# First products in another order, PLE's last weight splits behind the x parts, and the first norm tile in two pieces

## The chip, the core and the metric

The kernel runs on one NeuronCore of a Trainium2 chip. The metric is the device time of one execution in microseconds (us). The engines in the rows are TensorE (PE; its weight loads are PEld), VectorE (DVE), ScalarE (ACT), GpSimd (POOL) and SyncE (SP). A row that ends in "q" (ACTq, SPq) is the issue of a DMA from that engine's queue.

## The reference, cut to what matters

A two-layer decoder trunk on 256 tokens of width 1024, in float32:

```python
def swiglu(x, w_gate, w_up, w_down):
    return (jax.nn.silu(x @ w_gate) * (x @ w_up)) @ w_down

for i in range(DEPTH):                      # DEPTH = 2
    x = layer_norm(DN_ALPHA * x + 0.5 * swiglu(x, ffn_w_gate[i, 0], ...), ln_g[i, 0], ln_b[i, 0])
    mix = mixer_ab(x, ...) if i % 2 == 0 else mixer_cd(x, ...)
    x = layer_norm(DN_ALPHA * x + mix, ln_g[i, 1], ln_b[i, 1])
    x = layer_norm(DN_ALPHA * x + 0.5 * swiglu(x, ffn_w_gate[i, 1], ...), ln_g[i, 2], ln_b[i, 2])
    x = x + jax.nn.sigmoid(x @ ple_w_gate[i]) * (p[i] @ ple_w_proj[i])
```

D_FF is 2816. The mixers project x with one combined weight matrix, run their recurrences on the pieces, and project back with a second one.

## The kernel before, in words

**Split products.** Each float32 operand is split into a high and a low part, and a product is three matmuls: high by high, high by low, low by high (`mm3`, L69). Of the weights, ACT casts the high part (`wh`, L61) and DVE subtracts it to get the low part (`wl`, L62). Of the activations, x is transposed by PE into a PSUM tile, ACT casts the high part out of it (`xh`, L112) and DVE makes the low part (`xl`, L113), both in `split_xT`.

**Weights.** All weights are one stream of units of 128x2048 (1 MB). `Weights.unit` (L45) takes the next one: SP loads it into a staging tile `wst` (two buffers), and each half of it becomes a pair wh_n_0, wl_n_0 and wh_n_1, wl_n_1. The names in the rows below carry the unit's number. `behind` (L90, and the table `g.w.behind`) adds an ordering edge: the cast and the split of unit n may not be placed before the named instruction on the same engine. `layer_norm` (L145) uses it to put unit `at + 1 + t` behind the split of its own tile t. Apart from such edges, the order on each engine comes from a scheduler that places the instructions when the kernel is built, after its own estimates of when each can start; each engine then runs its list in that order.

**One half-layer.** The 256 tokens are two tiles (t = 0, 1) of 128. `ffn_body` (L198) makes the gate and up products of 11 column groups f, the hidden activations, and the down products into four PSUM accumulators, and ends in `layer_norm` (L117) of both tiles. `layer_norm` adds the residual (`r_ln`, L126), takes mean and variance (L129, L131; the power -0.5 on POOL, L81), subtracts and scales by the first row (L136) and makes x by the second (`x_ln`, L138), 512 columns at a time. Each half of 512 columns is transposed by four PE instructions into one PSUM tile (`tp_ln`, L142, tag "tr", two buffers for the whole kernel) and split. The next half-layer's first products need these splits.

**First products.** `run_tiles` (L163) makes one 128x512 output group for both token tiles out of two weight units (kh = 0, 1: rows k = 0 to 3 and 4 to 7 of x). With `tile_major` it runs all 24 products of tile 0 and then those of tile 1, so that tile 0 can start before tile 1 is normalised. It is used for f = 0 of each of the four feed-forward layers (`gu_f`) and for the first projection of each mixer (`pj_u` after norm 0, `pj_hq` after norm 3). For each half unit of rows, the products of xh with wh and wl come first and those of xl with wh last (L176).

**PLE.** `ple` (L280) makes the gate of the per-layer embedding in two column halves c for both tiles; `finish` (L297) applies it to x, transposes the 512 columns and splits them for the next layer. The last layer (`last`) has no such split. The places that the text speaks of are called after the norm or layer: ln0 to ln5 are the six norms (`ln3` is the first norm of the second layer), `ple0` is the first PLE, and f00, f01, f10, f11 are the feed-forward layers. Of the rest of the kernel, `nws_glr` (L595) is the high part of a small weight `nw_glr` of the second mixer, loaded on ACT's DMA queue (L591).

## Time and profile before

| | |
|---|---|
| three timed runs | 1224.89, 1226.21, 1229.82 us; median 1226.21 |
| the profiled execution | 1226.01 us, of which the span from first to last instruction is 1224.2 |
| PE busy | 1189.6 us, 97% of the span |
| DVE, ACT busy | 852.3 us (70%), 588.5 us (48%) |
| HBM traffic | 219.56 MB read, 12.06 MB written, 189 GB/s over the span |

The profile is one execution. A timeline row gives the start and the length of an instruction, what it writes and reads, and, in brackets, how long its engine sat idle before it and what ended that. Matmul lengths overlap: a 128x512 product is listed with 0.39 us but the next one starts 0.23 us after it. The column PEclk is the share of TensorE's full clock that was granted in a stretch: 1.00 is 2.4 GHz, 0.50 is 1.2 GHz.

### The profile page before, as it was taken

How to read it: one execution, taken by the hardware profiler on the slowest of the kernel's cores; microseconds unless marked ns; L12 is line 12 of the kernel's file. 1: busy time of each engine (PE TensorE's matmuls, PEld its weight loads, DVE VectorE, ACT ScalarE, POOL GpSimd, SP SyncE). 2: the span in 40 equal slices, each digit the busy share in tenths (PEclk: the TensorE clock that was granted, in tenths of full speed). 3: DMA queues.
4: the chain of work that ended last, by engine and by line, in shares of the span. 5: the costliest groups of instructions: out<-in, count | busy, mean ns of one | idle time of the engine just before them, and what ended most of it. 6: DMA issues, size and time to landing. Idle time of an engine off the chain costs nothing.

```text
span 1224.2 us, 17248 instructions
## 1 busy us (share of the span) xinstructions
PE 1189.6 (97%) x6786; PEld 987.4 (81%) x6786; DVE 852.3 (70%) x1352; ACT 588.5 (48%) x870; POOL 73.2 (6%) x126
## 2 busy tenths in 40 slices
PE   8999999999999999999999999999999999999998
PEld 6887777798878878888887888887888868888886
DVE  6999874779999675554576545456689876555566
ACT  5644443444666434444434444443575535444434
POOL 0011112120212000000000000000100100000000
PEclk9999999899999999999999999999999999999999
DMA  7567667587744546555526555554633327555532
GB/s 282 207 228 257 223 205 290 211 271 239 198 122 143 192 153 226 201 176 194 203 95 240 196 190 188 185 193 158 241 113 128 104 99 254 176 202 174 203 138 103
DMA packets 44609, 232.74 MB, mean 190 GB/s; under 512 B 9680, under 2 KB 10352, under 8 KB 20848
## 3 DMA queue, kind: packets, MB, share of 16 engines
q1 hardware_dynamic: 30672, 206.06, 48.5%
q0 software_dynamic: 4688, 14.16, 3.7%
q10 hardware_dynamic: 9168, 11.42, 2.9%
q8 instruction: 53, 0.87, 0.3%
q14 instruction: 28, 0.23, 0.1%
HBM read 219.56 MB, written 12.06 MB: 189 GB/s over the span
## 4 chain that ended last, share of the span: by engine, by line
PE 67%; DVE 10%; DMA 2%; ACT 2%; issue 1%; ACTq 0%; DVEq 0%
PE gu_f L178 29%; PE acc_f L72 5%; PE acc_f L70 5%; PE acc_f L71 5%; DVE wl L62 3%; DMA wst<-in_wall_dram 1%; PE acc_ab L72 1%; PE acc_ab L70 1%; PE acc_ab L71 1%; PE ht_f L215 1%; PE pj_u L178 1%; PE pj_hg L178 1%; PE pj_gr L178 1%; PE pj_hi L178 1%; PE pj_gv L178 1%
## 5 line engine op out<-in xcount | busy, mean ns | idle before, releaser
L62 DVE TENSOR_TENSOR wl<-wst,wh 128x1024 fp32r<-128x1024 f32 (+1 forms) x378 | 453.0, 1217 | 258.2 <-ACT wh L61 251.0
L61 ACT CAST wh<-wst 128x1024 fp32r<-128x1024 f32 (+1 forms) x378 | 385.9, 1045 | 349.2 <-PE acc_f L72 104.6
L70 PE MATMUL acc_f<-wh,hh_f 128*128 128x512 f32 x352 | 137.3, 391 | 1.9 <-ACT wh L61 1.4
L71 PE MATMUL acc_f<-wl,hh_f 128*128 128x512 f32 x352 | 137.5, 392 | 0.0
L72 PE MATMUL acc_f<-wh,hl_f 128*128 128x512 f32 x352 | 135.2, 392 | 0.0
L70 PEld LDWEIGHTS acc_f<-wh,hh_f 128*128 128x128 f32 x352 | 66.1, 188 | 15.8 <-ACT wh L61 1.6
L178 PE MATMUL gu_f<-wh,xh_in 128*128 128x512 f32 x176 | 71.9, 413 | 6.0 <-ACT wh L61 6.0
L72 PEld LDWEIGHTS acc_f<-wh,hl_f 128*128 128x128 f32 x352 | 66.1, 188 | 13.7
L71 PEld LDWEIGHTS acc_f<-wl,hh_f 128*128 128x128 f32 x352 | 66.1, 188 | 13.5
L178 PE MATMUL gu_f<-wh,xh_ple 128*128 128x512 f32 x176 | 70.8, 402 | 2.6 <-ACT xh_ple L112 2.6
L178 PE MATMUL gu_f<-wh,xh_ab 128*128 128x512 f32 x176 | 69.8, 396 | 0.5 <-ACT xh_ab L112 0.5
L178 PE MATMUL gu_f<-wl,xh_in 128*128 128x512 f32 x176 | 70.2, 402 | 0.0
L178 PE MATMUL gu_f<-wl,xh_ab 128*128 128x512 f32 x176 | 68.8, 391 | 1.3 <-DVE wl L62 1.3
L178 PE MATMUL gu_f<-wh,xh_cd 128*128 128x512 f32 x176 | 69.9, 397 | 0.0
L178 PE MATMUL gu_f<-wl,xh_ple 128*128 128x512 f32 x176 | 69.6, 396 | 0.0
L178 PE MATMUL gu_f<-wl,xh_cd 128*128 128x512 f32 x176 | 68.8, 391 | 0.7 <-DVE wl L62 0.7
L211 ACT ACTIVATE sg_f<-gu_f 128x256 f32<-128x256 f32 x88 | 33.7, 383 | 69.1 <-PE gu_f L178 67.8
L178 PE MATMUL gu_f<-wh,xl_ab 128*128 128x512 f32 x176 | 66.9, 391 | 0.0
L178 PE MATMUL gu_f<-wh,xl_cd 128*128 128x512 f32 x176 | 66.8, 391 | 0.0
L178 PE MATMUL gu_f<-wh,xl_ple 128*128 128x512 f32 x176 | 66.7, 391 | 0.0
L178 PE MATMUL gu_f<-wh,xl_in 128*128 128x512 f32 x176 | 66.6, 392 | 0.0
L212 DVE TENSOR_TENSOR sg_f<-sg_f,gu_f 128x256 f32<-128x256 f32 x88 | 36.8, 418 | 27.8 <-ACT sg_f L211 27.7
(469 smaller groups left out, 2348.9 us busy)
## 6 DMA issues: line engine op xcount, KB each, us to landing
wst<-in_wall_dram SPq DMA_DIRECT2D x185, 1024.0 KB, 4.8
row<-in_lnr_dram SPq DMA_DIRECT2D x12, 512.0 KB, 6.4
s5d<-s5pk POOLq DMA_DIRECT2D x8, 704.0 KB, 4.3
tab<-s5d ACTq DMA_DIRECT2D x8, 384.0 KB, 4.7
Q<-s5d ACTq DMA_DIRECT2D x8, 320.0 KB, 4.5
wst<-in_wall_dram SPq DMA_DIRECT2D x4, 512.0 KB, 6.7
s5d<-s5W POOLq DMA_DIRECT2D x8, 256.0 KB, 2.5
W<-s5d ACTq DMA_DIRECT2D x8, 256.0 KB, 4.0
```

What stands on the lines that cost most here:

```text
L61: ops = [nc.scalar.copy(wh[:, c], src[:, c])]
L62: ops.append(nc.vector.tensor_tensor(wl[:, c], src[:, c], f32(wh[:, c]), op=ALU.subtract))
L70: nc.tensor.matmul(out, xh, wh, start=first, stop=False)
L71: nc.tensor.matmul(out, xh, wl, start=False, stop=False)
L72: nc.tensor.matmul(out, xl, wh, start=False, stop=last)
L178: nc.tensor.matmul(ps[t], x, w, start=kh == 0 and i == 0, stop=kh == 1 and i == len(mms) - 1)
L211: nc.scalar.activation(sg, ps[t][:, 0:256], AF.Silu)
L212: nc.vector.tensor_tensor(sg, sg, ps[t][:, 256:512], op=ALU.mult)
L215: nc.tensor.transpose(tp[:, k, :], sg[:, k * P:(k + 1) * P], g.ident)
```

## The change

Three edits. (1) In `run_tiles` with `tile_major`, the 24 products of a tile are put in three lists: xh by wh of all eight rows of x together with xh by wl of the first unit; then xl by wh of all eight; then xh by wl of the second unit. (2) In `ple`'s `finish` for c = 1, the next weight units but one are put behind the x split of tile 0 and tile 1 (for the first PLE: units 100 and 101). (3) In `layer_norm`, the first 512 columns of tile 0 are scaled, transposed and split in two pieces of 256 columns; both pieces go into one PSUM tile. The parameter n of `layer_norm` is renamed, since n is now the number of blocks in a piece.

```diff
--- before.py
+++ after.py
@@ -104,20 +104,20 @@
     return [x[:, k, t * P:(t + 1) * P] for x in xT]
 
 
-def split_xT(g, t, half, src, xT):
-
-    nc = g.nc
-    s = slice(4 * half, 4 * half + 4)
+def split_xT(g, t, half, src, xT, part=slice(0, 4)):
+
+    nc = g.nc
+    s = slice(4 * half + part.start, 4 * half + part.stop)
     h, l = (x[:, s, t * P:(t + 1) * P] for x in xT)
     a = nc.scalar.copy(h, src)
     b = nc.vector.tensor_tensor(l, src, f32(h), op=ALU.subtract)
     g.anchors = a.ins, b.ins
 
 
-def layer_norm(g, n, t, acc, coef, xT):
-
-    nc = g.nc
-    name = f"ln{n}_{t}"
+def layer_norm(g, ln, t, acc, coef, xT):
+
+    nc = g.nc
+    name = f"ln{ln}_{t}"
     r = g.lnp.tile([P, D], F32, tag="ln_r", name=f"r_{name}")
     st = g.small.tile([P, 2, 6], F32, tag="ln_st", name=f"st_{name}")
     half = [slice(512 * h, 512 * h + 512) for h in range(2)]
@@ -133,14 +133,17 @@
     x = g.xp.tile([P, D], F32, tag=f"x{t}", name=f"x_{name}")
     for h in range(2):
         s = half[h]
-        nc.vector.scalar_tensor_tensor(r[:, s], r[:, s], mv[:, 0:1], g.grow[n][0][:, s], op0=ALU.subtract,
+        nc.vector.scalar_tensor_tensor(r[:, s], r[:, s], mv[:, 0:1], g.grow[ln][0][:, s], op0=ALU.subtract,
                                        op1=ALU.mult)
-        op = nc.vector.scalar_tensor_tensor(x[:, s], r[:, s], rstd, g.grow[n][1][:, s], op0=ALU.mult, op1=ALU.add)
-        g.scaled = (op.ins,)
         tp = g.ps.tile([P, 4, P], F32, tag="tr", name=f"tp_{name}_{h}", bufs=2)
-        for k in range(4):
-            nc.tensor.transpose(tp[:, k, :], x[:, (4 * h + k) * P:(4 * h + k + 1) * P], g.ident)
-        split_xT(g, t, h, tp, xT)
+        n = 4 if t or h else 2
+        for k0 in range(0, 4, n):
+            c = slice((4 * h + k0) * P, (4 * h + k0 + n) * P)
+            op = nc.vector.scalar_tensor_tensor(x[:, c], r[:, c], rstd, g.grow[ln][1][:, c], op0=ALU.mult, op1=ALU.add)
+            g.scaled = (op.ins,)
+            for k in range(k0, k0 + n):
+                nc.tensor.transpose(tp[:, k, :], x[:, (4 * h + k) * P:(4 * h + k + 1) * P], g.ident)
+            split_xT(g, t, h, tp[:, k0:k0 + n, :], xT, slice(k0, k0 + n))
     g.x[t] = x
     g.w.behind[g.w.at + 1 + t] = g.anchors
 
@@ -172,16 +175,26 @@
             c = slice(512 * (j % 2), 512 * (j % 2) + 512)
             h, l = of_tile(xT, t, k)
             mms += [(h, wh[:, c]), (h, wl[:, c]), (l, wh[:, c])]
-        if tile_major:
-            mms = [m for i, m in enumerate(mms) if i % 3 < 2] + mms[2::3]
         for i, (x, w) in enumerate(mms):
             nc.tensor.matmul(ps[t], x, w, start=kh == 0 and i == 0, stop=kh == 1 and i == len(mms) - 1)
 
     if tile_major:
         units = [g.w.unit() for kh in range(2)]
         for t in range(NT):
-            for kh in range(2):
-                part(kh, t, units[kh])
+            mms = [[], [], []]
+            for k in range(KT):
+                wh, wl = units[k // 4][k % 4 // 2]
+                c = slice(512 * (k % 2), 512 * (k % 2) + 512)
+                h, l = of_tile(xT, t, k)
+                mms[0].append((h, wh[:, c]))
+                if k < 4:
+                    mms[0].append((h, wl[:, c]))
+                else:
+                    mms[2].append((h, wl[:, c]))
+                mms[1].append((l, wh[:, c]))
+            mms = sum(mms, [])
+            for i, (x, w) in enumerate(mms):
+                nc.tensor.matmul(ps[t], x, w, start=i == 0, stop=i == len(mms) - 1)
         return
     for kh in range(2):
         pieces = g.w.unit()
@@ -310,6 +323,8 @@
         for k in range(4):
             nc.tensor.transpose(tp[:, k, :], xn[t][:, (4 * c + k) * P:(4 * c + k + 1) * P], g.ident)
         split_xT(g, t, c, tp, xT)
+        if c:
+            g.w.behind[g.w.at + 1 + t] = g.anchors
 
     for kh in range(2):
         units[0][kh] = g.w.unit()
```

The scheduler places the instructions anew around these edits. Three places follow. The first is PE from the transposes of norm 3's tile 0 (`tp_ln3_0_0` is its first 512 columns, `tp_ln3_0_1` its second) into the mixer's first projection `pj_hq_0`; wh_132, wl_132 are the first weight unit, wh_133, wl_133 the second. Before:

```order
L142 MATMUL tp_ln3_0_0_7784<-cs_217,x_ln3_0_7781 128x128 x4
L142 MATMUL tp_ln3_0_1_7793<-cs_217,x_ln3_0_7781 128x128 x4
L178 MATMUL pj_hq_0_7867<-wh_132_0_7871,xh_f10_7743 128x512
L178 MATMUL pj_hq_0_7867<-wl_132_0_7872,xh_f10_7743 128x512
...
L178 MATMUL pj_hq_0_7867<-wh_132_1_7875,xh_f10_7743 128x512
L178 MATMUL pj_hq_0_7867<-wl_132_1_7876,xh_f10_7743 128x512
...
L178 MATMUL pj_hq_0_7867<-wh_132_0_7871,xl_f10_7744 128x512 x2
L178 MATMUL pj_hq_0_7867<-wh_132_1_7875,xl_f10_7744 128x512 x2
L178 MATMUL pj_hq_0_7867<-wh_133_0_7881,xh_f10_7743 128x512
L178 MATMUL pj_hq_0_7867<-wl_133_0_7882,xh_f10_7743 128x512
```

and with the change:

```order
L145 MATMUL tp_ln3_0_0_7792<-cs_217,x_ln3_0_7790 128x128 x2
L145 MATMUL tp_ln3_0_1_7804<-cs_217,x_ln3_0_7790 128x128 x4
L197 MATMUL pj_hq_0_7879<-wh_132_0_7883,xh_f10_7752 128x512
L197 MATMUL pj_hq_0_7879<-wl_132_0_7884,xh_f10_7752 128x512
...
L145 MATMUL tp_ln3_0_0_7792<-cs_217,x_ln3_0_7790 128x128 x2
L197 MATMUL pj_hq_0_7879<-wh_132_1_7887,xh_f10_7752 128x512
L197 MATMUL pj_hq_0_7879<-wl_132_1_7888,xh_f10_7752 128x512
...
L197 MATMUL pj_hq_0_7879<-wh_133_0_7893,xh_f10_7752 128x512 x2
L197 MATMUL pj_hq_0_7879<-wh_133_1_7897,xh_f10_7752 128x512 x2
L197 MATMUL pj_hq_0_7879<-wh_132_0_7883,xl_f10_7753 128x512 x2
...
L197 MATMUL pj_hq_0_7879<-wl_133_0_7894,xh_f10_7752 128x512 x2
L197 MATMUL pj_hq_0_7879<-wl_133_1_7898,xh_f10_7752 128x512 x2
```

The eight transposes were in one run; now the second pair of `tp_ln3_0_0` comes after four products. The products with wh_133 now come ahead of those with xl, and the four with wl_133, which stood among them, are the last of the tile. The second place is ACT over the same stretch, before:

```order
L591 DMA nw_glr_8100<-in_cdlr_dram 128x128
L112 CAST xh_f10_7743<-tp_ln3_0_0_7784 128x4x128
L112 CAST xh_f10_7743<-tp_ln3_0_1_7793 128x4x128
L61 CAST wh_133_0_7881<-wst_133_7879 128x1024
L61 CAST wh_133_1_7885<-wst_133_7879 128x1024
L1238 DMA gup_8124<-in_cdgu_dram 32x256
L595 CAST nws_glr_8102<-nw_glr_8100 128x8x16
L1055 COPY ev_hq_0_7937<-pj_hq_0_7867 128x512
```

and with the change:

```order
L606 DMA nw_glr_8112<-in_cdlr_dram 128x128
L112 CAST xh_f10_7752<-tp_ln3_0_0_7792 128x2x128
L112 CAST xh_f10_7752<-tp_ln3_0_1_7804 128x4x128
L61 CAST wh_133_0_7893<-wst_133_7891 128x1024
L61 CAST wh_133_1_7897<-wst_133_7891 128x1024
L1253 DMA gup_8136<-in_cdgu_dram 32x256
L610 CAST nws_glr_8114<-nw_glr_8112 128x8x16
L112 CAST xh_f10_7752<-tp_ln3_0_0_7792 128x2x128
L1070 COPY ev_hq_0_7949<-pj_hq_0_7879 128x512
```

The cast of the first 512 columns was one instruction ahead of the two weight casts; of its two pieces, the second now stands behind both weight casts, a DMA issue and the cast of `nws_glr`. The same order, without `nws_glr`, is found at norms 0, 1 and 4: the second piece of xh comes behind the two weight casts of the second unit on ACT, and the second piece of xl behind their splits on DVE. The third place is ACT at the end of the first PLE (`xh_ple0` is the next layer's x; `tp_ple0_0_1` is tile 0, second half). Before:

```order
L61 CAST wh_100_0_6441<-wst_100_6439 128x1024
L302 ACTIVATE sg_ple0_0_512_6366<-acc_ple0_0_1_6227 128x512
L61 CAST wh_100_1_6445<-wst_100_6439 128x1024
L61 CAST wh_101_0_6521<-wst_101_6519 128x1024
L112 CAST xh_ple0_6230<-tp_ple0_0_0_6304 128x4x128
L112 CAST xh_ple0_6230<-tp_ple0_1_0_6315 128x4x128
L302 ACTIVATE sg_ple0_1_512_6401<-acc_ple0_1_1_6229 128x512
L61 CAST wh_101_1_6525<-wst_101_6519 128x1024
L112 CAST xh_ple0_6230<-tp_ple0_0_1_6370 128x4x128
L61 CAST wh_102_0_6555<-wst_102_6553 128x1024
L61 CAST wh_102_1_6559<-wst_102_6553 128x1024
```

and with the change:

```order
L61 CAST wh_99_1_6444<-wst_99_6438 128x1024
L315 ACTIVATE sg_ple0_0_512_6375<-acc_ple0_0_1_6236 128x512
L112 CAST xh_ple0_6239<-tp_ple0_0_0_6313 128x4x128
L112 CAST xh_ple0_6239<-tp_ple0_1_0_6324 128x4x128
L315 ACTIVATE sg_ple0_1_512_6410<-acc_ple0_1_1_6238 128x512
L112 CAST xh_ple0_6239<-tp_ple0_0_1_6379 128x4x128
L61 CAST wh_100_0_6450<-wst_100_6448 128x1024
L61 CAST wh_100_1_6454<-wst_100_6448 128x1024
L112 CAST xh_ple0_6239<-tp_ple0_1_1_6414 128x4x128
L61 CAST wh_101_0_6530<-wst_101_6528 128x1024
L61 CAST wh_101_1_6534<-wst_101_6528 128x1024
```

The first two x casts stood behind the casts of units 100 and 101; now they stand ahead of them, and units 100 and 101 come behind the second casts of tile 0 and tile 1. In all, DVE has 12 instructions more (six scalings and six splits), ACT six casts more and three loads of an activation table less, PE as many as before. In the first mixer (from norm 0 to norm 1) the scheduler also moved many instructions that the edits do not name, on PE, ACT and DVE.

## Rows read from the trace of the kernel before

**Rows 1.** Page, part 1: busy time, share, instructions of each engine.

```profile
PE 1189.6 (97%) x6786; PEld 987.4 (81%) x6786; DVE 852.3 (70%) x1352; ACT 588.5 (48%) x870; POOL 73.2 (6%) x126
```

**Rows 2.** What PE waited for: us in total, times, longest.

```profile
PE tp_ln L142 <- DVE x_ln L138: 3.5, 3, 1.7
PE gu_f L178 <- ACT xh_ple L112: 2.6, 1, 2.6
PE gu_f L178 <- DVE wl L62: 2.1, 2, 1.3
PE pj_z L178 <- DVE bc L817: 1.9, 1, 1.9
PE pj_hq L178 <- DVE wl L62: 1.6, 1, 1.6
```

**Rows 3.** Windows: length, busy of PE, PEld, DVE, ACT, POOL, PEclk, DMA.

```profile
221.25:228.08 6.83, 6.19 (x17) 4.63 (x16) 6.83 (x12) 4.25 (x5) 0.99 (x1) 0.50 0.96 315
...
299.75:303.16 3.41, 3.41 (x9) 2.67 (x8) 3.41 (x8) 0.05 (x1) 0.00 (x0) 0.50 0.74 231
...
664.98:668.39 3.41, 3.41 (x10) 2.67 (x9) 3.41 (x6) 1.50 (x3) 0.00 (x0) 0.50 0.30 127
...
1000.40:1004.00 3.60, 3.55 (x18) 2.72 (x19) 3.60 (x7) 2.85 (x4) 0.00 (x0) 1.00 0.00 0
```

**Rows 4.** PE's timeline at the end of ple0: start, length, instruction.

```profile
661.38 0.39 PE L71 MATMUL acc_ple<-wl,xh_f 128*128 128x512 f32 x1
661.61 0.39 PE L72 MATMUL acc_ple<-wh,xl_f 128*128 128x512 f32 x1
```

**Rows 5.** ACT's timeline at the end of ple0.

```profile
663.03 1.04 ACT L61 CAST wh<-wst 128x1024 fp32r<-128x1024 f32 x1 [3.42 <-DMA wst<-in_wall_dram]
663.98 1.07 ACT L112 CAST xh_ple<-tp_ple 128x512 fp32r<-128x512 f32 x2
```

**Rows 6.** PE's timeline from norm 3 into pj_hq.

```profile
853.51 0.50 PE L178 MATMUL pj_hq<-wh,xh_f 128*128 128x512 f32 x1 [0.24 <-ACT xh_f L112]
...
858.37 0.50 PE L178 MATMUL pj_hq<-wl,xh_f 128*128 128x512 f32 x1 [1.60 <-DVE wl L62]
...
861.22 1.04 PE L142 MATMUL tp_ln<-cs,x_ln 128*128 128x128 f32 x8
```

**Rows 7.** ACT's timeline over the same stretch.

```profile
852.44 0.37 ACTq L591 DMA_DIRECT2D nw_glr<-in_cdlr_dram  x1
...
853.83 2.01 ACT L61 CAST wh<-wst 128x1024 fp32r<-128x1024 f32 x2
857.30 0.30 ACT L595 CAST nws_glr<-nw_glr 128x128 fp32r<-128x128 f32 x1 [1.45 <-DMA nw_glr<-in_cdlr_dram]
```

**Rows 8.** DVE's timeline over the same stretch.

```profile
854.45 0.68 DVE L113 TENSOR_TENSOR xl_f<-tp_ln,xh_f 128x512 fp32r<-128x512 f32 x1
...
857.10 2.35 DVE L62 TENSOR_TENSOR wl<-wst,wh 128x1024 fp32r<-128x1024 f32 x2
```

**Rows 9.** Lines by form, 256 columns: busy, mean ns, idle before.

```profile
L218 DVE TENSOR_TENSOR hl_f<-ht_f,hh_f 128x256 fp32r<-128x256 f32 x88 | 34.6, 419 | 16.4 <-ACT hh_f L218 16.3
...
L218 ACT CAST hh_f<-ht_f 128x256 fp32r<-128x256 f32 x88 | 30.0, 369 | 28.5 <-PE ht_f L215 28.3
```

**Rows 10.** PE's timeline from norm 4 into f11.

```profile
1000.40 1.29 PE L142 MATMUL tp_ln<-cs,x_ln 128*128 128x128 f32 x8 [1.58 <-DVE x_ln L138]
1001.71 0.50 PE L178 MATMUL gu_f<-wh,xh_cd 128*128 128x512 f32 x1
...
1005.69 0.50 PE L178 MATMUL gu_f<-wl,xh_cd 128*128 128x512 f32 x1 [0.73 <-DVE wl L62]
...
1009.04 1.07 PE L142 MATMUL tp_ln<-cs,x_ln 128*128 128x128 f32 x6 [0.26 <-DVE x_ln L138]
```

**Rows 11.** DVE's timeline at norm 4.

```profile
999.51 1.41 DVE L138 SCALAR_TENSOR_TENSOR x_ln<-r_ln,rs_r_ln,row 128x512 f32<-128x512 f32 x2
1000.84 1.28 DVE L126 SCALAR_TENSOR_TENSOR r_ln<-acc_cd,x_ln 128x512 f32<-128x512 f32 x2
```

## The prediction

> **What bounds the kernel now.** Read first the busy shares: PE works 97% of the span, DVE 70%, ACT 48% [rows 1]. So the end is set by PE's own work, which the change leaves as it is, plus what PE loses in gaps. The second view is therefore the list of what PE waited for [rows 2]. After the start-up, its longest entries are the places that the edits touch: transposes that wait for a norm's x (three, 3.5 us), first products that wait for a low weight part (2.1 in two, and 1.6 at `pj_hq`), and the first product after ple0 (2.6). The third view is the granted clock by windows. Three stretches after the start ran at 0.50, that is at 1.2 GHz [rows 3]: the first follows the transposes' 1.7 us wait at ln0, the second the 1.9 us wait of `pj_z`, the third the 2.6 us wait after ple0 [rows 2]. The 1.58 us gap ahead of ln4's transposes was followed by no such stretch: the window behind it has 1.00 [rows 3, 10]. So I count a slow stretch behind a gap as long as those three, and none behind one no longer than the last. In 3.41 us at half the clock PE does 1.7 us of work, so a stretch costs 1.7 us on top of its gap.
>
> **The sum** is made against the profiled execution, 1226.01 us (span 1224.2 and 1.8 around it); the median of the three runs, 1226.21, stands 0.2 above, so both serve. Products start 0.23 us apart [rows 4].
>
> *ple0 into f10 (second edit).* PE's last two products start at 661.38 and 661.61 [rows 4]. The first cast of the new x starts only at 663.98, since ACT runs wh_101_0 ahead of it, which waited for its load until 663.03 [rows 5]; the product follows 0.6 us later. With the change nothing stands ahead of the cast. It overwrites the buffer of the old x, whose last high-part reader is the product at 661.38; that ends at 661.77, the cast starts at about 661.85 and the first product at 662.5 instead of 664.6. That gives 2.1 us, and the gap falls to 0.5, so the slow stretch at 664.98 goes too: 1.7. What is late next is unit 100. From its first product (f) PE has 16 products with unit 99 and eight transposes, 3.7 + 0.8 us, and wants wh_100 at f + 4.5. ACT casts tile 0's second half when its four transposes are out, at f + 4.4, 0.5 to the next instruction, and then wh_100_0, 1.04 us [rows 5]: f + 5.95. That is a new wait of 1.5, and the splits of unit 100 on DVE, which stand behind the same x part, add 0.5 between the products. Term: -2.1 - 1.7 + 2.0 = -1.8. Bounds: -3.8 if the wait is hidden, +0.4 if only the gap of 2.1 is won, the slow stretch stays and the wait grows by half a microsecond.
>
> *ln3 into pj_hq (edits one and three).* First the gain. The first cast is of 256 columns, 0.37 us [rows 9] instead of 0.59, so the first product starts at about 853.2 instead of 853.51 [rows 6]. And the wait of 1.60 us for wl_133_0 [rows 6] goes, since products with wl_133 are now last. Then the loss. After four products PE stands at 854.3 before the second pair of transposes. These go into the same PSUM tile as the first pair and wait until DVE has taken the low part out of it. DVE comes to that at 854.45 [rows 8], 0.42 for 256 columns [rows 9]; the pair runs at 854.9 to 855.2. The products of the second piece wait for its cast, and that stands on ACT behind two weight casts (2.0 us) and the cast of `nws_glr`, whose load is issued at 852.44 and lets it start at 857.30 [rows 7]. That cast was of no account before: ACT's idle 1.45 us ahead of it cost nothing, because nothing that PE needed stood behind it. Now the piece's cast starts at about 857.5, and the first product at 857.9. PE's gap is 2.7 us. Twenty products remain, 4.6 us: tile 0 ends at 862.5, against 861.22 [rows 6]. That is +1.3, and the gap is longer than all three that were followed by a slow stretch: +1.7. Term: +3.0. Bounds: -1.9 if the piece's cast is not late (0.3 and 1.6 won), +4.7 if a second slow stretch follows, as after ln0, where it lasted 6.83 us [rows 3].
>
> *ln4 into f11 (the same edits).* The x scaling is two steps of 0.7 us from 999.51 on [rows 11], and PE waits for the first until 1000.40 [rows 10]. With 256 columns the first transposes run at 1000.1, the first product at 1000.9 instead of 1001.71. Then come four products, four transposes and the second pair, up to 1002.75. ACT casts the other half at 1002.6, then two weight casts until 1005.0, then the piece; the product is at 1005.4. Gap: 2.65. Ten products later, at 1007.7, PE needs the low part of the piece. On DVE, from 999.51 on, it stands behind the x scaling (1.4) and r_ln (1.3) [rows 11], the split of the first piece (0.4) [rows 9], two statistics of 0.6 each (estimated from the steps beside them), the split of the other half (0.6), two weight splits (2.35) [rows 8] and two steps like the scaling (1.4), which the order now puts ahead of wl_151_1; its own 0.4 ends at 1008.5. That is another wait of 0.8. Ten products remain: 1010.9, against 1009.04 [rows 10]. Here the removed wait of 0.73 [rows 10] is contained. So +1.9; a slow stretch after the gap adds 1.7, of which 0.8 falls into the wait for DVE. Term: +2.8. Bounds: -1.7 with no late piece, +4.5.
>
> *ln0 and ln1.* By the same steps: at ln0 the first product is 0.7 earlier, but the second piece's cast leaves PE idle for about 1.0 inside the slow stretch that is there anyway: +0.5. At ln1 the removed wait of 1.3 [rows 2] and 0.4 from the shorter cast stand against a wait of 1.5 for the second piece, with small waits that go too: -0.4. Term: +0.1, from -1.0 to +3.5 (each could start or prolong a slow stretch).
>
> *At nothing.* ln2 and ln5: twelve products of the PLE's projection lie between the pieces and cover the later cast. f00's first products: the start is bound by the first load and its slow clock, and wl_1 was not waited for. The twelve more steps on DVE (two of 0.42 instead of one of 0.68 [rows 8, 9]) and six on ACT: beside 30% idle on DVE, where it is not part of the waits above. Three table loads less: ACT is idle half the time. The moved instructions of the first mixer: the trace does not show them, and they concern one wait of 1.9 with its stretch; one that I can follow (the last tap of `bc1` is now ahead of wl_45_0 on DVE) shortens that wait, and others, such as gate products that no longer lie between the score products, lay waits open. From -3.6 (that wait and its stretch gone) to +3.6 (one like it more); I take 0, as the instructions moved are many, in both directions.
>
> Sum: -1.8 + 3.0 + 2.8 + 0.1 = +4.1, so 1230.1, and 1230.0 is what I predict.
>
> A page of the Trainium skill speaks against the third edit: "PSUM — Partial Sum Buffer", section "PSUM bank collisions raise a hardware error", says that PE may not write a bank while ACT or DVE reads it, even at other columns, and that software must keep them apart. Two pieces of 512 columns' transposes fill one such bank, so the second pair must wait for the readers of the first. In the trace of before, four transposes always went out in one run, so no run so far shows it; the new order does have the wait. Were the pieces free of each other, the sum would be that of the last rival below.
>
> **Rivals.** (a) *The clock holds and the mixer's wait goes.* The gaps at ln3 and ln4 fall so that no slow stretch follows (-1.7 and -0.9), and the `pj_z` wait shrinks by 1.5 us and loses its own (-1.5 - 1.7). For it: a gap of 1.58 went unpunished, and the tap moved. Against: 2.7 is well above 1.9. Time: 1230.1 - 5.8 = 1224.3.
>
> (b) *Slow stretches double.* PE idles twice within a few microseconds at ln3 (0.6 and 2.7), ln4 (0.6, 2.65, 0.8) and f10 (1.5 and 0.5). If the clock stays at half for 6.83 us, as at ln0 [rows 3], behind ln3 and ln4, that adds 1.7 at each, and if one follows f10's wait, 1.7 more: 1235.2, slower than before by 0.7%. For it: the one double stretch stands at a norm, with two gaps (1.7 and 0.6). Against: ple0's single gap of 2.6 had 3.41 only. It decides from the point where the second gap falls into the slow stretch of the first.
>
> (c) *The pieces are in time* (the edits do what they say and no more): the casts wait for neither `nws_glr` nor the weight casts. Then ln3 is -1.9 and ln4 -1.7: 1230.1 - 4.9 - 4.5 = 1220.7. Against it is the order on ACT; for it only that `nws_glr`'s load could land sooner.
>
> **How the numbers follow.** Forecast 0.55, with a range of its own from 1226.5 to 1233.5; (a) 0.20; (b) 0.19; (c) 0.06. A measurement of this kernel can tell about 0.5%, 6.1 us, from no change: faster is under 1220.1, slower over 1232.3. Faster: half of (c) and a little of (a), 0.06. Slower: (b) and the upper part of the forecast's range, 0.27. The rest, 0.67, is the same. The range reaches from (c)'s edge over (a) to just above (b): 1221.5 to 1236.5.
>
> **What would show it.** Right: PE's list has no wait for wl at `pj_hq`, and instead one of about 2.7 us for xh at `pj_hq` and one of 2.6 at f11's `gu_f`, each followed by a window at 0.50; the wait after ple0 is 0.5 us, no window at 0.50 follows it, and a wait of 1.5 for wh stands 4.5 us later. Wrong: no wait for xh behind the first four products (rival c), a full clock behind them (a), or the sum of PE's gaps after ln0 to ln1 differing by more than 3 us (the mixer, taken as 0).

## The result: slower by 0.7%, and the profile after

The changed kernel takes 1236.85 us (median of five, 1231.96 to 1238.02) against 1226.21: ratio 1.0067, interval [1.0046, 1.0088]. (A ratio here is estimated from the runs of both kernels, with its 95% interval; it is not the quotient of the two medians, which is 1.0087 for this pair.) Run again beside a second set of the kernel before, it takes 1235.83 us against 1227.61: 1.0076 [1.0049, 1.0103]. The forecast of 1230.0 had the sign of its sum right and too small a size; its likeliest verdict, no change by its own bar of 0.5%, was wrong. The first median lies 0.35 us above the range, the second inside it.

The first profile is that of the fastest run (1231.96 us, span 1230.2; last product 5.7 us later than before); that of the second measurement is of a run of 1235.75 us (last product 9.5 us later). Where one profile has a number and the other another, both are given.

The busy times of the page hardly move [rows 1]:

```profile
PE 1192.9 (97%) x6786; PEld 988.7 (80%) x6786; DVE 855.7 (70%) x1364; ACT 586.9 (48%) x873; POOL 72.6 (6%) x126
```

What PE waited for, us in total, times, longest (the first entry includes the start, 5.9):

```profile
PE gu_f L197 <- ACT wh L61: 7.9, 4, 5.9
PE tp_ln L145 <- DVE x_ln L142: 3.6, 3, 1.6
PE gu_f L197 <- ACT xh_cd L112: 3.1, 3, 2.4
PE pj_hq L197 <- ACT xh_f L112: 2.3, 3, 1.8
...
PE tp_ln L145 <- DVE xl_f L113: 0.4, 1, 0.4
PE gu_f L197 <- ACT xh_ple L112: 0.4, 1, 0.4
...
PE pj_z L179 <- DVE bc L832: 0.3, 1, 0.3
```

The waits for wl at `pj_hq` and `gu_f` are gone, and that for `xh_ple` fell from 2.6 to 0.4 us [rows 2]. In their place stand waits for xh, 1.8 us at `pj_hq` and 2.4 at f11.

PE's timeline at ple0, norm 3 and norm 4 (start, length, instruction, in brackets the idle time before it):

```profile
662.78 0.50 PE L197 MATMUL gu_f<-wh,xh_ple 128*128 128x512 f32 x1 [0.44 <-ACT xh_ple L112]
...
668.81 0.50 PE L197 MATMUL gu_f<-wh,xh_ple 128*128 128x512 f32 x1 [1.18 <-ACT wh L61]
...
853.46 0.44 PE L145 MATMUL tp_ln<-cs,x_ln 128*128 128x128 f32 x2 [0.45 <-DVE xl_f L113]
855.72 0.50 PE L197 MATMUL pj_hq<-wh,xh_f 128*128 128x512 f32 x1 [1.82 <-ACT xh_f L112]
...
860.50 1.04 PE L145 MATMUL tp_ln<-cs,x_ln 128*128 128x128 f32 x8
...
1004.73 1.49 PE L145 MATMUL tp_ln<-cs,x_ln 128*128 128x128 f32 x6
1008.62 0.80 PE L197 MATMUL gu_f<-wh,xh_cd 128*128 128x512 f32 x1 [2.41 <-ACT xh_cd L112]
```

ACT's timeline over the two norms:

```profile
850.97 0.38 ACTq L606 DMA_DIRECT2D nw_glr<-in_cdlr_dram  x1
...
852.13 2.00 ACT L61 CAST wh<-wst 128x1024 fp32r<-128x1024 f32 x2
855.10 0.30 ACT L610 CAST nws_glr<-nw_glr 128x128 fp32r<-128x128 f32 x1 [0.96 <-DMA nw_glr<-in_cdlr_dram]
855.30 0.36 ACT L112 CAST xh_f<-tp_ln 128x256 fp32r<-128x256 f32 x1
...
1006.30 1.99 ACT L61 CAST wh<-wst 128x1024 fp32r<-128x1024 f32 x2
1008.20 0.37 ACT L112 CAST xh_cd<-tp_ln 128x256 fp32r<-128x256 f32 x1
```

At both norms the cast of the second piece is the last of a row: behind two weight casts at norm 4, behind two and the cast of `nws_glr`, itself waiting for its load, at norm 3. The product of k = 2, the first that reads the second piece (k counts the blocks of 128 columns of x), starts 0.42 us after that cast starts.

Windows on the stretches at half the clock, and one behind the gap at `pj_hq` (length, busy of PE, PEld, DVE, ACT, POOL, granted clock, DMA):

```profile
223.00:226.41 3.41, 3.02 (x10) 1.81 (x8) 3.41 (x7) 2.72 (x4) 0.00 (x0) 0.50 1.01 329
328.81:332.22 3.41, 3.41 (x70) 3.41 (x69) 3.41 (x6) 1.55 (x3) 0.00 (x0) 0.50 0.74 290
926.14:932.97 6.83, 6.83 (x21) 5.53 (x20) 6.02 (x10) 4.46 (x7) 0.00 (x0) 0.50 0.17 73
1004.65:1011.48 6.83, 4.42 (x14) 3.36 (x13) 6.68 (x13) 2.75 (x4) 0.93 (x1) 0.50 0.08 17
857.00:860.50 3.50, 3.50 (x16) 2.67 (x15) 2.38 (x4) 0.00 (x0) 2.50 (x3) 1.00 0.77 225
```

Together 20.5 us at 0.50, against 13.7 before [rows 3]. The second profile has 23.9; its two late stretches are

```profile
928.19:935.02 6.83, 6.83 (x23) 5.72 (x23) 5.25 (x10) 3.73 (x7) 0.00 (x0) 0.50 0.24 103
1006.70:1016.94 10.24, 7.83 (x22) 5.99 (x21) 8.17 (x14) 2.75 (x4) 0.94 (x1) 0.50 0.34 82
```

The stretch at 926 us lies in the second mixer, 70 us behind the gap at `pj_hq`, and PE is busy all through it. That at 1004.65 begins 1.6 us before the gap at f11 (1006.21 to 1008.62): it follows the 1.55 us that the transposes waited for x and only six instructions of PE after that, and the gap lies inside it.

### The profile page after: what moved, and what is told of

It is laid out like the page before. It is cut to its first block, busy times and chain, and to the rows that moved or that the text cites. A ratio compares the mean times of both kernels' runs of the same rounds, so it can differ in the third digit from the quotient of the medians.

```text
span 1230.2 us, 17269 instructions
## 1 busy us (share of the span) xinstructions
PE 1192.9 (97%) x6786; PEld 988.7 (80%) x6786; DVE 855.7 (70%) x1364; ACT 586.9 (48%) x873; POOL 72.6 (6%) x126
## 5 line engine op out<-in xcount | busy, mean ns | idle before, releaser
L179 PE MATMUL gu_f<-wh,xh_in 128*128 128x512 f32 x160 | 64.2, 401 | 0.0
L179 PE MATMUL gu_f<-wh,xh_ple 128*128 128x512 f32 x160 | 63.4, 397 | 0.0
L179 PE MATMUL gu_f<-wh,xh_ab 128*128 128x512 f32 x160 | 63.3, 396 | 0.0
L179 PE MATMUL gu_f<-wh,xh_cd 128*128 128x512 f32 x160 | 63.3, 396 | 0.0
L179 PE MATMUL gu_f<-wl,xh_in 128*128 128x512 f32 x160 | 62.7, 392 | 0.0
L179 PE MATMUL gu_f<-wh,xl_ab 128*128 128x512 f32 x160 | 62.5, 391 | 0.0
L179 PE MATMUL gu_f<-wh,xl_ple 128*128 128x512 f32 x160 | 62.4, 390 | 0.0
L179 PE MATMUL gu_f<-wl,xh_ple 128*128 128x512 f32 x160 | 62.3, 389 | 0.0
L179 PE MATMUL gu_f<-wl,xh_ab 128*128 128x512 f32 x160 | 62.3, 389 | 0.0
L179 PE MATMUL gu_f<-wl,xh_cd 128*128 128x512 f32 x160 | 62.3, 389 | 0.0
```

The source lines that it names most:

```text
L179: nc.tensor.matmul(ps[t], x, w, start=kh == 0 and i == 0, stop=kh == 1 and i == len(mms) - 1)
```

## The experiments

Every profile is cut at the same PE instructions: the first transpose of norm 0, the first transpose of the pieces `ct_u0` behind `pj_u`, norm 1's first transpose, the first product of the PLE, norm 3's first transpose, norm 4's, and the first product of f11's second group. The table gives how much longer than before each stage is, from the start of one such instruction to the start of the next, in us, and the time at half clock between the start-up and the last product (before: 13.7). Each column is one profile; e0 is the changed kernel's second one. A half-clock stretch of 3.41 us that comes or goes is 1.7 of a stage. Profiles of one list differ too: after, e0 and e14 have the same lists up to norm 3, and their first three stages together are +.6, +2.6 and +4.6. So a difference of a us or two in one column is no finding by itself.

| stage (us before) | after | e0 | e14 | e3 | e9 | e11 | e13 | e5 | e1 | e8 | e12 | e7 | e10 |
|---|---|---|---|---|---|---|---|---|---|---|---|---|---|
| f00 (220.4) | +1.3 | +3.8 | +2.4 | -1.7 | -.9 | +.2 | -1.5 | +1.3 | +2.6 | +3.8 | +3.1 | -.5 | -.4 |
| ln0, pj_u (16.3) | -1.4 | -1.4 | +.3 | +1.1 | +.5 | +.3 | +.1 | +4.3 | -1.2 | -.4 | -.7 | -.2 | +.9 |
| first mixer (205.2) | +.7 | +.2 | +1.9 | +3.8 | +1.0 | -.3 | -.4 | -.5 | +6.1 | +6.5 | +6.9 | +.1 | -.4 |
| ln1, f01 (196.4) | -.9 | -.9 | -1.0 | -.2 | -1.0 | -1.0 | -1.0 | +1.2 | -1.0 | 0 | -1.0 | -1.0 | -1.0 |
| ple0, f10 (213.8) | -1.1 | -1.1 | -1.2 | -3.1 | -1.9 | -1.9 | -1.9 | -1.6 | -2.4 | -2.8 | -1.9 | -1.9 | -2.2 |
| ln3, second mixer (148.2) | +3.9 | +4.0 | -1.1 | +4.0 | +5.3 | +2.5 | +.5 | -.1 | -1.0 | -.1 | -1.2 | -.3 | -1.2 |
| ln4, f11 (15.8) | +3.1 | +4.7 | +1.5 | +3.9 | +3.1 | +.5 | +.4 | +1.3 | 0 | 0 | 0 | 0 | 0 |
| rest (203.2) | +.1 | +.2 | +.1 | +.2 | -.1 | 0 | -.1 | +1.9 | 0 | -.1 | 0 | 0 | 0 |
| sum | +5.7 | +9.5 | +3.0 | +7.9 | +6.0 | +.2 | -3.7 | +7.8 | +3.1 | +6.9 | +5.4 | -3.8 | -4.3 |
| at half clock | 20.5 | 23.9 | 13.7 | 17.1 | 20.5 | 20.5 | 13.7 | 13.7 | 10.2 | 17.1 | 17.1 | 6.8 | 10.2 |

Times below are medians; the ratios compare with runs of the kernel before that were taken on the same chip. The runs were made on four chips (e1, e3, e5, e12; e0, e7, e8, e9; e10, e11, e13; e14), and runs of one kernel on one chip spread by 3 to 13 us, so across these groups the ratios are compared and not the medians.

**One edit at a time.** The first edit alone, on the kernel before:

```diff
-            for kh in range(2):
-                part(kh, t, units[kh])
+            mms = [[], [], []]
...
+            for i, (x, w) in enumerate(sum(mms, [])):
+                nc.tensor.matmul(ps[t], x, w, start=i == 0, stop=i == len(mms) - 1)
```

> Only the first edit (order of the first products), on the kernel before. Theory A (the loss comes from the two pieces sharing one PSUM tile, which puts piece 2's cast behind weight casts): this kernel has no pieces, so it is at 1222 to 1227 us; the waits of pj_hq and gu_f for wl (1.6 and 2.1 us in the profile before) are gone. Theory B (no edit in particular: any new order of the program moves the half-clock stretches, and there are more of them now): 1230 to 1237 us at a mean clock near .988. Theory C (the new order of products itself costs): 1228 to 1231 us with the clock as before, the time lost inside the first products.

1231.66 us, ratio 1.0036 [1.0016, 1.0055]. Theory A named the wrong range: with no pieces in it this kernel is slower. But the mean clock is .992, and .993 in the runs of before beside it, so B's reason isn't there either. C's range is missed by .7 us, and the time is lost elsewhere than it said (see e12). The wl waits fell to .4 us each, as A said.

The third edit alone:

```diff
-        for k in range(4):
...
-        split_xT(g, t, h, tp, xT)
+        n = 4 if t or h else 2
+        for k0 in range(0, 4, n):
...
+            split_xT(g, t, h, tp[:, k0:k0 + n, :], xT, slice(k0, k0 + n))
```

> Only the third edit (two pieces in one PSUM tile), on the kernel before. Theory A: 1230 to 1237 us, with gaps of 1.5 to 3 us in front of k = 2 of the first products at pj_hq and at f11, released by ACT's cast of piece 2. Theory B: 1230 to 1237 us too, but with the extra time in half-clock stretches that follow no such gap. Theory C: 1222 to 1227 us.

1234.21 us, 1.0052 [1.0033, 1.0071]. Both A and B named this range; the gaps are those of A, 2.36 us at `pj_hq` (855.22 to 857.58) and 2.41 at f11 (1008.18 to 1010.59). A half-clock stretch follows the first, another begins 2.7 us ahead of the second, and a third lies in the second mixer:

```profile
858.71:862.12 3.41, 3.41 (x9) 2.33 (x8) 2.00 (x4) 0.00 (x0) 2.10 (x3) 0.50 0.86 211
930.39:933.80 3.41, 3.41 (x10) 2.62 (x10) 3.41 (x8) 2.62 (x5) 0.00 (x0) 0.50 0.17 70
1005.48:1008.89 3.41, 2.70 (x10) 1.90 (x8) 2.88 (x6) 1.10 (x2) 0.00 (x0) 0.50 0.00 0
```

The first two edits without the third:

```diff
-            for kh in range(2):
-                part(kh, t, units[kh])
+            mms = [[], [], []]
...
+        if c:
+            g.w.behind[g.w.at + 1 + t] = g.anchors
```

> The first two edits without the pieces. Theory A: 1220 to 1225 us, faster than both kernels; no xh or wl wait over 1 us at pj_hq, f11 keeps the one wait for its norm. Theory B: 1230 to 1237 us at a mean clock near .988. Theory C: 1227 to 1230 us.

1230.89 us, 1.0041 [1.0020, 1.0061]. Again not A's range. The table shows why both e1 and e12 missed it: from f01 on they gain 4.4 and 4.0 us, and before that they lose 7.5 and 9.3, in f00 and in the first mixer. (About half of the gain, that at ple0, is not the edit's, as e8 shows below.) There the edit leaves the products as many as they were; what changes is how the scheduler places the mixer's instructions among and behind f00's and `pj_u`'s products. That gave theory D, stated with the next run.

**The new order early and late.** Old order at f00 and `pj_u`, new order from f01 on, second edit kept:

```diff
+        old = not (g.w.at >= 60)
...
+            if old:
+                for kh in range(2):
+                    part(kh, t, units[kh], True)
+                continue
```

> The first two edits, but the new order of products only at f01, f10, pj_hq and f11; the engines' lists up to the end of the first mixer are those of before. Theory D (the order of products gains after the first mixer, as the profiles of e1_order_only and e12_no_pieces show stage by stage: .9 us at f01, 1.9 to 2.4 around ple0, .95 at pj_hq, and what these two lose, they lose in f00 and in the first mixer, which the scheduler lays out anew): 1220.5 to 1224 us, faster than both kernels. Theory B (half-clock stretches move with any change and decide): 1226 to 1232 us, with more half-clock time than the 13.7 us of before.

1223.12 us, 0.9973 [0.9951, 0.9996]: faster than both kernels, as D said. The waits for wl of 1.3 us at f01 [rows 2] and 1.60 at `pj_hq` [rows 6] are .39 and .40. The reverse, the new order at f00 and `pj_u` alone:

```diff
-        old = not (g.w.at >= 60)
+        old = not (g.w.at < 60)
```

> The first edit at f00 and pj_u alone, the later first products as before. Theory D: 1230 to 1235 us, 4 to 8 us over before, the loss between the start and the end of the first mixer, idle time of that mixer near 11 us where before has 6.6; from f01 on each stage within .5 us of before. Theory B: 1226 to 1232 us with no stage in particular; if the order of products has nothing to do with the first mixer's layout, 1226 to 1227.5.

1232.93 us, 1.0051 [1.0033, 1.0070], in D's range, and from norm 1 on within .1 us of before in each stage but one. That one, ple0 and f10, is 2.8 us shorter, where D had named .5 at most: behind ple0 the gap is 1.2 us shorter and no slow stretch follows it.

```profile
671.71 1.04 ACT L61 CAST wh<-wst 128x1024 fp32r<-128x1024 f32 x1 [2.15 <-PE acc_ple L71]
...
673.29 0.50 PE L178 MATMUL gu_f<-wh,xh_ple 128*128 128x512 f32 x1 [1.40 <-ACT xh_ple L112]
```

In this stage the lists of PE, ACT and DVE are, instruction for instruction, those of before, so no edit made the difference. The load of the unit whose cast stands ahead of the x cast took 4.6 us from issue to landing here and 5.9 in the profile of before; in e1 and e10, where ACT has the same order at this place, it took 4.7 and 5.0, the gap is 1.3 and 1.6, and no slow stretch follows either. So 1.2 us of the 2.6 [rows 2] and the stretch behind it [rows 3] are not the price of ACT's order, which all four share, and the table's gains at ple0 are gains over a late load. Against e8 this stage is 1.7 us longer in the changed kernel, .9 in e7 and .6 in e10.

The first mixer's main part (first product of `pj_z` to norm 1) in four profiles, same columns as above, of before, e7, e1 and e8:

```profile
298.76:441.99 143.23, 138.53 (x1066) 118.28 (x1067) 122.35 (x240) 77.70 (x132) 19.94 (x30) 0.99 0.53 169
```

```profile
298.03:441.40 143.37, 138.28 (x1067) 118.65 (x1067) 122.40 (x240) 77.76 (x132) 21.02 (x30) 0.99 0.53 169
```

```profile
300.53:449.51 148.98, 138.99 (x1067) 118.66 (x1067) 124.50 (x243) 76.90 (x132) 18.60 (x30) 0.99 0.52 168
```

```profile
187.35:190.76 3.41, 3.22 (x8) 2.54 (x9) 3.41 (x6) 1.73 (x5) 0.00 (x0) 0.50 0.61 238
301.18:451.90 150.72, 140.65 (x1068) 119.52 (x1067) 124.70 (x243) 76.78 (x132) 18.61 (x30) 0.98 0.51 166
```

The reader sees PE's busy time unchanged up to the clock, and its idle time (length less busy) go from 4.7 and 5.1 us to 10.0 and 10.1. The row at 187 us is the half-clock stretch inside f00; all seven profiles with the new order at f00 are 1.3 to 3.8 us longer there, and five have this stretch; of the seven without (before among them) none is longer by over .2, and one has it (e11, at 184.5). Another part of f00's loss lies right behind the first products, where PE transposes the first hidden activations:

```profile
21.78 0.44 PE L232 MATMUL ht_f<-cs,sg_f 128*128 128x128 f32 x2 [0.48 <-DVE sg_f L229]
```

This wait is .48 us in all seven with the new order; of the other seven, e11 has .62, e13 .24 and five none. In the changed kernel, where the pieces make the scheduler lay out the mixer in a third way, the mixer's loss is only .2 to .7 (1.9 in e14, with the same lists there).

e10 is e7 without the second edit:

```diff
-        if c:
-            g.w.behind[g.w.at + 1 + t] = g.anchors
```

> As e7_late_12 without the second edit: unit 100's cast stands ahead of the x splits at ple0 again. In e1_order_only the two stages from acc_ple0 to gu_f10_2 took 1.30 and 1.10 us less than before, in e12_no_pieces 2.18 less and .30 more, so the second edit costs .5 us in all: theory D says 1220 to 1223.5 us, .5 below e7_late_12's 1223.1 and within what can be told apart from it. If the second edit brings what the forecast gave it (1.8 us at ple0): 1224 to 1226 us, with the wait of 2.6 us for xh_ple back.

1224.30 us, 0.9983 [0.9967, 1.0000]; against e7's 0.9973 no difference can be told. The median lies in the other theory's range, .8 us above D's, but the wait is not that theory's 2.6. In the stages around ple0 it is .3 us better than e7. So the second edit shows no gain there: what it wins in front of f10 (the wait for `xh_ple` is 1.6 us in e10, .4 in e7), the wait for unit 100 takes back.

**What the pieces cost.** e7 with the third edit at norms 3 and 4 alone, so that all up to norm 3 stays in its order:

```diff
+        n = 4 if t or h or ln not in (3, 4) else 2
```

> As e7_late_12, with the third edit (two pieces in one PSUM tile) at ln3 and ln4 alone. The first mixer is again that of before, so the difference to e7_late_12 is the price of the pieces at these two norms. Theory A/D: 5 to 9 us over e7_late_12 (in e3_pieces_only the two stages took 4.4 and 3.9 us more than before; e12_no_pieces .95 less and the same), with gaps of 1.8 to 2.4 us in front of k = 2 at both and a half-clock stretch behind at least one. If the pieces are harmless: within 2 us of e7_late_12.

1230.46 us, 1.0026 [1.0015, 1.0037], 7.3 us over e7, as A and D said. Its gaps:

```profile
855.06 0.80 PE L204 MATMUL pj_hq<-wh,xh_f 128*128 128x512 f32 x1 [2.00 <-ACT xh_f L112]
...
1009.20 0.80 PE L204 MATMUL gu_f<-wh,xh_cd 128*128 128x512 f32 x1 [2.41 <-ACT xh_cd L112]
```

Next, two ways to take the second piece out of its place. A PSUM tile of its own for each piece, in the changed kernel:

```diff
-        tp = g.ps.tile([P, 4, P], F32, tag="tr", name=f"tp_{name}_{h}", bufs=2)
...
+            tp = g.ps.tile([P, 4, P], F32, tag="tr", name=f"tp_{name}_{h}_{k0}", bufs=2)
```

> The changed kernel with a PSUM tile of its own for each piece (the third tile of a norm then waits for the first piece's split). Piece 2's cast now stands in front of the weight casts on ACT at every norm. Theory A: the gaps in front of k = 2 at pj_hq (1.82 us) and at f11 (2.41 us) fall under 0.6 us each, and the time is 1221 to 1228 us. Theory B: the gaps fall, but the time stays at 1231 to 1237 us since half-clock stretches come elsewhere.

1234.24 us, 1.0059 [1.0038, 1.0080]. The gaps in front of k = 2 are gone. But the time is B's and not A's, and not for B's reason, since there are 13.7 us at half clock as before. A norm's tile 0 now fills three tiles out of two buffers, and the third, the second half of x, needs the buffer of the first piece, when its low part is made. Its transposes now stand behind eight products. At norm 4, PE and ACT:

```profile
1007.81 0.60 PE L145 MATMUL tp_ln<-cs,x_ln 128*128 128x128 f32 x4
1010.03 0.73 PE L197 MATMUL gu_f<-wh,xh_cd 128*128 128x512 f32 x2 [1.62 <-ACT wh L61]
```

```profile
1008.45 0.58 ACT L112 CAST xh_cd<-tp_ln 128x512 fp32r<-128x512 f32 x1 [2.24 <-PE tp_ln L145]
1008.93 2.00 ACT L61 CAST wh<-wst 128x1024 fp32r<-128x1024 f32 x2
```

So the wait moved from k = 2 to k = 4, and the two norms in front of the PLEs lost 1.6 us each as well (waits of 1.0 for xl and .6 for wl).

The other way is ACT's order. In e9, unit 133 at norm 3 and unit 151 at norm 4 are put behind the second piece (their casts on ACT behind its cast, and their splits on DVE behind its split):

```diff
+            if k0:
+                piece2 = g.anchors
...
-    g.w.behind[g.w.at + 1 + t] = g.anchors
+    g.w.behind[g.w.at + 1 + t] = g.anchors + piece2
```

> As e9_late_12_pieces, with the weight unit at + 1 (133 at ln3, 151 at ln4) put behind the casts and splits of piece 2 too; nws_glr, which waits for its DMA, stands right ahead of piece 2's cast at ln3. If the weight casts in the queue are what holds piece 2 at f11: its gap of 2.41 us falls under .8 us and stage tp_ln4 to gu_f11_1 is within 1.5 us of before (e9: +3.1). If it is the shared tile alone: the gap stays over 1.5 us. At ln3 the gap of 2.0 us stays, since nws_glr is still ahead, and 1 to 2 us of waiting for unit 133 come on top. Time 1226 to 1231 us.

1227.38 us, 1.0001 [0.9982, 1.0020]. PE's two gaps, and ACT at norm 3:

```profile
854.75 0.80 PE L207 MATMUL pj_hq<-wh,xh_f 128*128 128x512 f32 x1 [2.10 <-ACT xh_f L112]
...
1003.68 0.50 PE L207 MATMUL gu_f<-wh,xh_cd 128*128 128x512 f32 x1 [0.52 <-ACT xh_cd L112]
```

```profile
854.13 0.30 ACT L620 CAST nws_glr<-nw_glr 128x128 fp32r<-128x128 f32 x1 [3.13 <-DMA nw_glr<-in_cdlr_dram]
854.34 0.37 ACT L112 CAST xh_f<-tp_ln 128x256 fp32r<-128x256 f32 x1
```

At f11 the weight casts were the cause: 2.41 falls to .52. At norm 3 the gap stands, as `nws_glr` and its load are still ahead. With that cast put behind too:

```diff
+    if name == "glr":
+        behind(g, op, g.piece2)
```

> As e11_weights_behind, with nws_glr's cast behind piece 2 too. Piece 2's cast is then next after the casts of piece 1 and of the second half at both norms. If ACT's order is the cause: gaps in front of k = 2 under .8 us at pj_hq and f11 both, up to 1 us of waiting for the weights instead, the half-clock stretches at 926 and 1005 us gone, and 1222 to 1226 us, not below e7_late_12. If the shared tile is the cause: gaps over 1.5 us stay, 1228 to 1231 us.

1223.41 us, 0.9978 [0.9960, 0.9995], by the ratios 6 us under e9 and level with e7. Of the forecast only one part missed: a half-clock stretch of 3.41 us at 923.0 remains. PE and ACT:

```profile
851.26 0.50 PE L209 MATMUL pj_hq<-wh,xh_f 128*128 128x512 f32 x1 [0.46 <-ACT xh_f L112]
...
999.82 0.50 PE L209 MATMUL gu_f<-wh,xh_cd 128*128 128x512 f32 x1 [0.53 <-ACT xh_cd L112]
```

```profile
850.84 0.37 ACT L112 CAST xh_f<-tp_ln 128x256 fp32r<-128x256 f32 x1 [1.68 <-PE tp_ln L146]
851.11 2.00 ACT L61 CAST wh<-wst 128x1024 fp32r<-128x1024 f32 x2
853.00 0.30 ACT L622 CAST nws_glr<-nw_glr 128x128 fp32r<-128x128 f32 x1
```

The weight casts begin 2.8 us behind the start of the first piece's cast instead of .75 in e9, and PE waits only .2 us for them. The pieces, freed of the queue, win nothing over e7.

**The changed kernel again, and with its queues mended.**

> The changed kernel once more, on the chip of these runs. 1234 to 1239 us. The gaps in front of k = 2 at pj_hq (1.82 us) and f11 (2.41 us) stand within .1 us, since they are in its queues. The half-clock stretch behind the gap at f11 is there again; the one at 926 us, which no gap precedes, is there again if the place of the stretches belongs to the program (B), and elsewhere or away if it is chance.

1235.83 us. The gap at f11 is 2.41 again, that at `pj_hq` 2.41 where the first profile had 1.82, so the latter isn't fixed by the order, and the .1 us named for it was missed. `nw_glr`'s load ends it: `nws_glr` was cast 4.13 us behind the load's issue in the first profile and 4.71 in this one (853.04 to 857.75). Both late stretches are at the same place of the program.

e14 is the changed kernel with the edits of e11 and e13 at norms 3 and 4:

```diff
+            if k0 and ln in (3, 4):
+                piece2 = g.anchors
```

> The changed kernel, with unit 133, unit 151 and nws_glr put behind piece 2's cast and split at ln3 and ln4, as in e13_all_behind; the engines' lists up to ln3 are those of the changed kernel. If ACT's order at these two norms is what the changed kernel loses by: its three stages from tp_ln3 to acc_cd and from tp_ln4 to gu_f11_1, 7.0 us over before in its profile and 9.1 in its second one, fall to 1 to 3 us over before, and the time to 1228 to 1232 us; what stays over before then is in f00 and in the half-clock stretches, as the lists up to ln3 are the same. If the pieces cost by something else: 1234 to 1238 us as the changed kernel.

1228.36 us, 1.0008 [0.9990, 1.0026], so the interval holds no change, where the changed kernel had 1.0076. Its gaps are .46 and .52 us:

```profile
858.29 0.50 PE L202 MATMUL pj_hq<-wh,xh_f 128*128 128x512 f32 x1 [0.46 <-ACT xh_f L112]
...
1006.49 0.49 PE L202 MATMUL gu_f<-wh,xh_cd 128*128 128x512 f32 x1 [0.52 <-ACT xh_cd L112]
```

The two stages that hold norms 3 and 4 went from +7.0 and +8.7 us to +.4, better than the 1 to 3 named, by the order of casts and splits at these two norms alone. The column's sum is +3.0 all the same, since its first three stages have +4.6 with the lists that gave +.6 and +2.6 in the changed kernel's profiles. A half-clock stretch of 3.41 us is left at norm 4, again ahead of the gap, at 1002.81; without it the two stages would be under those of before.

## Why the prediction was right or wrong

*ple0 into f10: the wait right, the gain not shown.* The wait for `xh_ple` is .44 (forecast .5), no half-clock window follows, and a wait for wh of 1.18 us begins 4.8 us behind the first product (forecast 1.5 at 4.5). Forecast -1.8, measured -1.1. But the term took the whole 2.6 us and the stretch behind them for the price of ACT's order, and about half of that was one late load: e8, whose lists are those of before here, has a gap of 1.40 and no stretch, and its stage is 1.7 us shorter than the changed kernel's. That the second edit wins here, as the term had it, is not shown; beside e8 and e10 it wins nothing.

*ln3 into pj_hq: the wait right, the slow stretch in another place.* The first edit's gain is there, the wait of 1.60 [rows 6] is gone, and the second piece waits behind `nws_glr`; the gap is 1.82 and 2.41, forecast 2.7. I took the load's 4.86 us from issue to cast before [rows 7]; it was 4.13 and 4.71 now. The half-clock stretch right behind it did not come in either profile of the changed kernel (the window from 857.00 has 1.00), though it did in e3, e9 and e11, behind or inside gaps of 2.0 to 2.4. Instead a stretch of 6.83 us came in the second mixer. +3.0 was forecast for the norm; the stage with the mixer has +3.9 and +4.0. The rule that I counted stretches by, one behind any gap of 1.7 us or more and none behind 1.58, fails both ways: none followed 1.82 and 2.41 us here, nor 1.71 us ahead of norm 4's transposes in e7, and at norm 0 one came behind 1.42 to 1.45 us and a second, shorter wait in all five profiles with pieces there.

*ln4 into f11: the wait right, the slow stretch mis-sized.* The gap is 2.41 (forecast 2.65). The stretch at half clock came before it, not behind it, so the transposes and products on both sides of the gap are slowed; it lasted 6.83 and 10.24 us, and the stage is +3.1 and +4.7 instead of +2.8. What I left out is that the pieces break up PE's work there before the gap: two transposes, four products, six transposes, with a wait of 1.55 us ahead of them and one of .46 among them. That this is the cause isn't shown, since e11 and e13 have the same row there without a stretch.

*The cause of both waits* was put down as ACT's order, with the shared PSUM tile ahead of it. The Trainium skill, "PSUM — Partial Sum Buffer", section "PSUM bank collisions raise a hardware error", says that PE must not write a bank that another engine reads. The trace agrees as far as the order goes: the second pair of transposes waited .45 us for DVE's read of the first pair's columns (853.46), and in e5, with two tiles, it did not. Whether the bank or the tile makes the program wait, no run tells apart. But that wait costs only .45; e13 and e14, and at f11 e11, which keep the tile and change the order of casts and splits, remove most of the rest.

*f00 at nothing: wrong.* This is the term that failed outright. It looked at the start of the first products, where only the first profile has a new wait over .2 us (.57 for wh); it did not look at what follows them, the transposes that now wait .48 us for `sg_f`, nor at the small products of the first mixer (`s5w`, `s5k`), which the scheduler places among f00's products from 72 us on and moved. +1.3 and +3.8, with the half-clock stretch at 187 us in the second profile. Which of the moved instructions costs the rest wasn't tried apart.

*First mixer at 0, ±3.6:* +.7 and +.2 (+1.9 in e14), right for this kernel. But with the first edit alone it is +6 to +7, outside the bounds, so the 0 was luck rather than insight. *ln0, ln1 at +.1:* the stages have -2.3 together. Of this, -1.4 is at ln0, where the half-clock stretch is 3.41 us instead of 6.83; e14, with 6.83, has +.3. The working of ln0, 1.0 us of idle time less 0.7, comes to +.3 and not +.5.

*The sum and the rivals.* +4.1 was forecast; the two profiles have +5.7 and +9.5, of which the half-clock time alone is 3.4 and 5.1 (half of 20.5 - 13.7 and of 23.9 - 13.7). By price the medians lie at rival (b), 1235.2: slow stretches that double. Of its three places (ln3, ln4, f10) one was right, f11 behind ln4; another stretch came 70 us behind `pj_hq`, and none came at f10. I gave (b) .19 because only one stretch of before had 6.83 us [rows 3]; the profile of before held too few gaps of this length to size what follows them.

## What to carry to other kernels

A reader that is cut in two stands twice in its queue, and the second half stands wherever the scheduler's estimate puts it: before cutting, see what is placed between the halves, and pin it behind the second (6 to 8 us here, by the ratios of e9 and e13 and of the changed kernel and e14). An edit that leaves the work alone can still cost through what the scheduler lays out anew far away, so try it in the places where the lists around it stay (e7 won .3% with the edits by which e12 lost .4%). A stage table cut at the same instructions shows in one view what the medians of such kernels hide. And a stage that comes out otherwise though no list in it changed (ple0 in e8, 2.8 us) shows how much of one profile belongs to that execution.

## What was not expected of the hardware

The granted clock fell to 0.50 in the second mixer, between 923 and 935 us, with PE busy throughout the stretch (6.83 of 6.83 us, or 3.41 of 3.41 in e3 and e13). That is so in five profiles, all of kernels with pieces at norm 3 (after, e0, e3, e9, e13); in e5, e11 and e14, with pieces too, and in the six without, it is not. e13 has it with a gap of only .46 at `pj_hq`, so the gap alone isn't its cause; what is stays open. Nor does the length of a gap tell what comes: behind (or, in e9 and e11, inside) 1.82 to 2.41 us at `pj_hq` a half-clock stretch came within 4 us in three of five profiles. At norm 4 one begins between the transposes' wait and the gap at f11 in five of the eight profiles with pieces there (after, e0, e3, e9, e14), in none of the six others, though their transposes waited as long (1.3 to 1.7 us); it lasted 3.41 us with the gap of .52 (e14) and 3.41 to 10.24 with that of 2.41.
